# Gate and up weights in 512 x 256 blocks, and prefix counts laid out by expert, in a two-layer MoE backbone

## The chip, the cores and the metric

The kernel runs on one core of one Trainium2 chip. The metric is device microseconds (us) for one execution of the whole program; less is better. Engines: PE (TensorE), DVE (VectorE), ACT (ScalarE), POOL (GpSimd), SP (the queue that issues most transfers).

## What is computed

Two layers over 2048 latent and 256 context tokens of width 1024. Each layer has an attention half and then an expert-choice MoE half, cut here to what matters:

```
aff = softmax(h @ w_router)                 # 16 experts
gate, idx = top_k(aff^T, cap)               # per expert: 256 latent tokens, 32 context tokens
xe = h[idx]                                 # gather
a = xe @ w_gate[e];  u = xe @ w_up[e]       # 1024 x 512 each
y = (silu(a) * u) @ w_down[e] * gate        # 512 x 1024
out = zeros.at[idx].add(y)                  # scatter-add
```

Context tokens take part in layer 0 only. All of it is float32, with products made of three float32r products (high x high, low x high, high x low).

## The kernel before

The program is recorded in one order; each engine runs its own instructions in that order, and a waiting instruction holds all those behind it on its engine.

**Weights** come through `Stream` (lines 111 to 221). A block is 128 partitions x 1024 float32, 512 KB. `_load` (L163) issues its transfer on SP into `wraw`; `_high` (L178) makes the high part `wh` on ACT; `_low` (L186) makes the low part `wl` on DVE and thereby frees the `wraw` buffer, of which there are six, for the next transfer. `next(key, ahead=6)` makes sure that the high parts of the six blocks behind the wanted one have been recorded:

```
        while len(self.split) <= min(i + ahead, self.end - 1):
            ...
            self._high()
```

So an ACT cast of a block stands in ACT's order when the block six places ahead of it is used, and everything that ACT does after it waits for that block's transfer.

**One expert** (loop at L1790) uses twelve blocks: for each of four column blocks of 128 a gate block and an up block, eight matmul triples each into the PSUM tiles `pa` and `pu` (L1802 to L1804), and then four down blocks (L1833 to L1840). A block of gate or up is 1024 rows x 128 columns, so that each run in DRAM is 512 bytes. `tick()` (after each of these blocks) lets waiting tasks record their next step: `act` (silu on ACT, product on DVE, `gh` on ACT, `gl` on DVE), `trans(e + 1)` (transposes of the next expert's gathered tokens on PE, L1571; `xh` on ACT, L1580; `xl` on DVE, L1584; two PSUM buffers `tr`), `choose(e + 2)` and `put` (gated rows, scatter-add by POOL, L1666).

**The prefix counts.** `route` writes, once a layer, for each expert the running count of chosen tokens, 2048 bf16 values, to DRAM (`PFX`, L1499; `PFC` for the context tokens). They lie as [8 pieces, 16 experts, 256]. `fetch(e)` (L1518) copies the 4096 bytes of one expert to all 128 partitions of `pb`: 512 KB written, in runs of 512 bytes. `choose(e)` compares them with the slot numbers (L1530, two passes of DVE), makes the token numbers `ix`, and POOL gathers the rows `xe` (L1546). `pb` has two buffers; `fetch(e + 1)` is issued at the end of `choose(e)` on SP, between the weight blocks.

At the start of each MoE half the order is route, fetch(0), fetch(1), choose(0), gather, transposes, first expert. In layer 0, PE meanwhile works on modulation columns (`mod_piece`, L393). Late in layer 1 the finishing tasks (`fin_tile`, L1742 to L1774: two ACT passes and two DVE passes of 1024 columns a tile, L1769 and L1773) run beside the last three experts, one step a tick, and after them.

Of the kernel before, what the change touches and what calls it, by code (L numbers as in the profile page):

```python
# [7 lines left out]
F32 = mybir.dt.float32  # L8
F32R = mybir.dt.float32r
BF = mybir.dt.bfloat16  # L10
I32 = mybir.dt.int32
AF = mybir.ActivationFunctionType
# [11 lines left out]
KD = D // 128  # L24
NE = 16
CAP = 256
CCAP = 32
# [54 lines left out]
STEP = object()  # L82
# [142 lines left out]
def build(ctx, tc, t, out):  # L225
    nc = tc.nc
    V, S, P, G, SY = nc.vector, nc.scalar, nc.tensor, nc.gpsimd, nc.sync
# [4 lines left out]
    T = Tasks()  # L232
    W = Stream(nc, tc, T)

    def bcast(ap, n=128):
        return bass.AP(tensor=ap.tensor, offset=ap.offset, ap=[[0, n], *ap.ap])
# [31 lines left out]
    def dr(name, shape, dt=F32):  # L268
        return [dram.tile(shape, dt, name=f"{name}{i}") for i in range(DEPTH)]
# [10 lines left out]
    H2 = [dram.tile([n, HX], F32, name=f"H2{n}") for n in (TT, SEQ)]  # L280
    ACC = dr("ACC", [SEQ, D])
    ACCC = dram.tile([CTX, D], F32, name="ACCC")
    PFX = dr("PFX", [8, NE, 256], BF)
    PFC = dr("PFC", [8, NE, 32], BF)
    X1 = dram.tile([TT, D], F32, name="X1")

    def xrows(l, i):
# [10 lines left out]
    def k8(w):  # L298
        return w.rearrange("(k p) c -> p k c", p=128)

    def whole(a):
        return lambda x: x.rearrange("p (k c) -> p k c", k=a)
# [4 lines left out]
    def add_mod(l, j, kind="split", halves=(0, 1)):  # L307
        for b in halves:
            W.add(("mod", l, j, b), [(whole(4), k8(t["w_mod"][l][512 * b:512 * b + 512, 256 * j:256 * (j + 1)]))], kind)

    def mod_beside(l, e):

        j = NMOD + e - 1
        return j if l == 0 and 1 <= e and j < NLATE else None
# [23 lines left out]

    def add_moe(l):
        for e in range(NE):  # L340
            for f in range(4):
                for z in "gu":
                    W.add((z, l, e, f), [(whole(8), k8(t["w_gate" if z == "g" else "w_up"][l, e][:, 128 * f:128 * (f + 1)]))])
                if f in (1, 2) and mod_beside(l, e) is not None:
                    add_mod(1, mod_beside(l, e), halves=(f - 1,))
            for j in range(2):
                for b in range(2):
                    W.add(("d", l, e, j, b), [(whole(2), k8(t["w_down"][l, e][256 * b:256 * b + 256, 512 * j:512 * (j + 1)]))])
# [1078 lines left out]
    def route(l, aff, sb, ps):  # L1427


        last = l == DEPTH - 1  # L1430
# [25 lines left out]
        for it in range(15):  # L1456
# [9 lines left out]
            pc = ps.tile([128, 512], F32, name="py")  # L1466
# [29 lines left out]
        V.tensor_copy(need[:, 2, :], pc[:, 0:nj])  # L1496
        for j, s in enumerate(parts):
            V.tensor_tensor_scan(px[:, s], gt[:, s], gt[:, s], need[:, 2, j:j + 1], ALU.add, ALU.bypass)
            SY.dma_start((PFX, PFC)[j][l].rearrange("a e n -> (a e) n"), px[:, s])  # L1499
        yield  # L1500


    def phase_moe(l, aff):
        es = ExitStack()
        last = l == DEPTH - 1
# [9 lines left out]
        def fetch(e):  # L1515

            pb = sb.tile([128, SEQ], BF, name="pb")
            SY.dma_start(pb.rearrange("p (a n) -> p a n", a=8), bcast(PFX[l][:, e, :]))  # L1518
            pc = None
            if not last:  # L1520
                pc = sb.tile([CCAP, 256], BF, name="pc")
                SY.dma_start(pc.rearrange("p (a n) -> p a n", a=8), bcast(PFC[l][:, e, :], CCAP))
            prefixes[e] = pb, pc

        def choose(e):
# [98 lines left out]
            fp = es.enter_context(tc.tile_pool(name="fin", bufs=1))  # L1624
            fg, fb = load_ln2(l, fp)

        def act(ff, pa, pu, gh, gl):
            yield STEP
            sa = sb.tile([128, NX], F32, name="sa", bufs=3)
            S.activation(sa, pa, AF.Silu)  # L1630
            yield
            V.tensor_tensor(sa, pu, sa, op=ALU.mult)
            yield
            S.copy(gh[:, ff, :NX], sa)
            yield
            yield
            V.tensor_tensor(gl[:, ff, :], sa[:, :CAP], gh.bitcast(F32)[:, ff, :CAP], op=ALU.subtract)
            if not last:
                V.tensor_tensor(gh[:, ff, NX:NX + CCAP], sa[:, CAP:], gh.bitcast(F32)[:, ff, CAP:NX], op=ALU.subtract)
# [43 lines left out]
        def tick():  # L1683
            T.tick()
            F.tick()
# [28 lines left out]
        def fin_early():  # L1714
            for _ in range(FINLAG):
                yield STEP
            for n in range(14 + 2 * FINK):
                e = E0 + (n - 16) // 2
                while n >= 16 and e not in flags:
                    yield STEP  # L1720
                yield from fin_next()
                if n < 16:
                    SY.dma_start(xs[n], ACC[1][128 * n:128 * n + 128, :])
                else:
                    fin_gather(e, n % 2, xs[n])
                F.add(fin_tile(n))
                for _ in range(1 if "end" in flags else FINSTEP if NE - 2 not in flags else FINSTEP2):
                    yield STEP
# [61 lines left out]
        for e in range(NE):  # L1790
            xh, xl, gates = xT[e]
            gh = one.tile([128, 4, CAP + 2 * CCAP], F32R, name="gh")
            gl = one.tile([128, 4, CAP], F32R, name="gl")
            for j in range(2):
                for f in range(2):
                    pa = ps.tile([128, NX], F32, name="pa")
                    pu = ps.tile([128, NX], F32, name="pu")
                    for pp, z in ((pa, "g"), (pu, "u")):
                        wh, wl = W.next((z, l, e, 2 * j + f), ahead=6)
                        for k in range(KD):  # L1800
                            cs_ = slice(128 * k, 128 * k + 128)
                            P.matmul(pp, wh[:, cs_], xh[:, k, :], start=(k == 0), stop=False)  # L1802
                            P.matmul(pp, wh[:, cs_], xl[:, k, :], start=False, stop=False)  # L1803
                            P.matmul(pp, wl[:, cs_], xh[:, k, :], start=False, stop=(k == KD - 1))  # L1804
                        if z == "g":
                            tick()
                    if mod_beside(l, e) is not None and 2 * j + f in (1, 2):
                        if j == 0:
                            piece = mod_piece(1, mod_beside(l, e), ps, sb, True, "py", 2, apart=True,
                                              room=lambda: sb.tile([128, NX], F32, name="sa", bufs=3))  # L1810
                        next(piece)
                    T.add(act(2 * j + f, pa, pu, gh, gl), True)
                    if j == 0 and f == 0 and e + 1 < NE:
                        T.add(trans(e + 1))
                    if last and j == 0 and f == 0 and e == E0:
                        F.add(fin_early())
                    if j == 1 and f == 0 and e + 2 < NE:
                        T.add(choose(e + 2))
                    tick()
            ys = {}  # L1820
            for j in range(2):
                pys, ws = {}, {}

                def down(a, f):
                    if a not in pys:
                        pys[a] = ps.tile([128, 512], F32, name="py")
                    if f // 2 not in ws:
                        ws[f // 2] = W.next(("d", l, e, j, f // 2))
                    s_ = slice(512 * (f % 2), 512 * (f % 2) + 512)
                    wh, wl = (z[:, s_] for z in ws[f // 2])  # L1830
                    if a < 2:
                        h, lo = (z[:, f, 128 * a:128 * a + 128] for z in (gh, gl))
                        P.matmul(pys[a], h, wh, start=(f == 0), stop=False)  # L1833
                        P.matmul(pys[a], h, wl, start=False, stop=False)
                        P.matmul(pys[a], lo, wh, start=False, stop=(f == 3))
                    else:

                        P.matmul(pys[a][:2 * CCAP], gh[:, f, CAP:CAP + 2 * CCAP], wh, start=(f == 0), stop=False,
                                 skip_group_check=True)
                        P.matmul(pys[a][:CCAP], gh[:, f, CAP:CAP + CCAP], wl, start=False, stop=(f == 3),  # L1840
                                 skip_group_check=True)

                if j == 0:
                    for a in range(2):
                        for f in range(3):
                            down(a, f)
                        tick()
                for a in range(2 if last else 3):
                    for f in range(3 if j == 0 and a < 2 else 0, 4):
                        down(a, f)  # L1850
                    T.add(put(e, 128 if a < 2 else CCAP, a, j, pys[a], ys, gates), True)
                    tick()
# [99 lines left out]
```

## Time and profile before

| | us |
|---|---|
| median of 3 runs | 4326.2 (4321.42 to 4334.8) |
| profiled execution, its own time | 4323.15 |
| its span, first to last instruction | 4321.4 |
| PE busy | 3853.9 (89%) |
| DVE busy | 2915.8 (67%) |
| ACT busy | 1999.0 (46%) |
| mean granted TensorE clock | 0.943 |

The time is that of the device; the span is that of the records within it. Times in rows are us from the span's start. Busy shares are means over stages with different limits. Layer 0's experts run from 1487.3 to about 2178 with the last one behind, layer 1's from 3570.5 to about 4259.

### The profile page before, as it was taken

The page shows a single profiled execution, that of the slowest core. Times are in us where ns is not written, and L with a number is a line of the kernel's source. Part 1 is how long each engine was busy: PE and PEld are TensorE (multiplying, and loading weights), DVE is VectorE, ACT ScalarE, POOL GpSimd, SP SyncE. Part 2 cuts the span into 40 slices and gives each one's busy share as a digit, 9 for nine tenths or more (in the row PEclk, how much of TensorE's full clock was granted, in tenths as well). Part 3 has the DMA queues.
Part 4 walks back from the last instruction along what each step waited for, and adds up shares of the span by engine and source line. Part 5 has one row for each costly group of instructions (what it writes and reads, how often), then busy time and mean ns, then how long its engine had stood idle before and what let it go on. Part 6 is the DMA issues. An engine that isn't in the chain of part 4 may idle for free. (4 is left out here: it accounts for less than half of the span.)

```text
span 4321.4 us, 64189 instructions
## 1 busy us (share of the span) xinstructions
PE 3853.9 (89%) x22980; PEld 3285.1 (76%) x22980; DVE 2915.8 (67%) x5836; ACT 1999.0 (46%) x3918; POOL 783.9 (18%) x850
## 2 busy tenths in 40 slices
PE   7999989999998699999978999899989918988893
PEld 5877778888885388888857888788878718888783
DVE  6555549998676366676747665499877756656576
ACT  4344338887332143343425443388763304333344
POOL 0000011052221022222210000111422201111114
PEclk9999989999998899999989999999999959999996
DMA  7666674586644878888857666645865327776796
GB/s 229 172 209 187 198 189 107 118 177 154 235 159 143 189 208 201 204 217 196 223 171 230 192 205 187 171 116 110 169 185 193 131 80 190 195 221 194 217 234 203
DMA packets 897295, 789.94 MB, mean 183 GB/s; under 512 B 125928, under 2 KB 780400, under 8 KB 893136
## 3 DMA queue, kind: packets, MB, share of 16 engines
q1 hardware_dynamic: 855744, 656.83, 56.4%
q0 software_dynamic: 41232, 129.01, 10.6%
q8 instruction: 182, 2.98, 0.3%
q14 instruction: 137, 1.12, 0.1%
HBM read 607.08 MB, written 178.48 MB: 182 GB/s over the span
## 5 line engine op out<-in xcount | busy, mean ns | idle before, releaser
L178 ACT CAST wh<-wraw 128x1024 fp32r<-128x1024 f32 x636 | 655.9, 1048 | 621.9 <-DMA wraw<-in_w_gate 278.2
L186 DVE TENSOR_TENSOR wl<-wraw,wh 128x1024 fp32r<-128x1024 f32 x636 | 754.7, 1217 | 152.2 <-ACT wh L178 152.0
L1190 DVE TENSOR_TENSOR pl<-pt,ph 128x256 fp32r<-128x256 f32 (+2 forms) x792 | 360.2, 495 | 23.0 <-ACT ph L1199 18.4
L1199 ACT CAST ph<-pt 128x256 fp32r<-128x256 f32 (+2 forms) x792 | 308.9, 445 | 99.2 <-PE pt L1087 91.3
L624 PE MATMUL gem<-hh,wh 128*128 128x512 f32 (+1 forms) x960 | 354.5, 369 | 0.0
L625 PE MATMUL gem<-hl,wh 128*128 128x512 f32 (+1 forms) x960 | 352.1, 367 | 0.0
L626 PE MATMUL gem<-hh,wl 128*128 128x512 f32 (+1 forms) x960 | 350.0, 365 | 0.0
L1070 ACT ACTIVATE p<-lg,mx 128x640 f32<-128x640 f32 (+3 forms) x408 | 331.5, 813 | 38.3 <-DVE mx L1062 36.7
L1802 PE MATMUL pa<-xh,wh 128*128 128x288 f32 (+1 forms) x1024 | 317.5, 310 | 0.0
L1804 PE MATMUL pa<-xh,wl 128*128 128x288 f32 (+1 forms) x1024 | 308.3, 301 | 0.8 <-DVE wl L186 0.8
L1803 PE MATMUL pa<-xl,wh 128*128 128x288 f32 (+1 forms) x1024 | 307.3, 300 | 0.0
L1802 PE MATMUL pu<-xh,wh 128*128 128x288 f32 (+1 forms) x1024 | 299.9, 293 | 0.0
L1804 PE MATMUL pu<-xh,wl 128*128 128x288 f32 (+1 forms) x1024 | 294.6, 288 | 0.0
L1803 PE MATMUL pu<-xl,wh 128*128 128x288 f32 (+1 forms) x1024 | 292.6, 286 | 0.0
L1666 POOL DMA_INDIRECT ACC<-y,ix x62 | 150.7, 2430 | 651.7 <-DVE y L1647 334.2
L802 PE MATMUL gem<-wh,hh 128*128 128x512 f32 x544 | 220.7, 406 | 0.6 <-ACT hh L593 0.6
L803 PE MATMUL gem<-wl,hh 128*128 128x512 f32 x544 | 217.6, 400 | 1.4 <-DVE wl L186 1.4
L804 PE MATMUL gem<-wh,hl 128*128 128x512 f32 x544 | 217.0, 399 | 0.0
L1833 PE MATMUL py<-wh,gh 128*128 128x512 f32 x512 | 205.1, 401 | 12.7 <-DVE y L1647 6.1
L1571 PE MATMUL tr<-ident,xe 128*128 128x128 f32 x512 | 89.6, 300 | 139.4 <-DVE xl L1584 91.8
L1802 PEld LDWEIGHTS pa<-xh,wh 128*128 128x128 f32 x1024 | 208.5, 204 | 3.1
L1546 POOL DMA_INDIRECT xe<-H,ix x80 | 98.2, 1228 | 619.9 <-DVE ix L1541 352.9
(352 smaller groups left out, 10103.4 us busy)
## 6 DMA issues: line engine op xcount, KB each, us to landing
wraw<-in_w_in SPq DMA_DIRECT2D x160, 512.0 KB
wraw<-in_w_gate SPq DMA_DIRECT2D x128, 512.0 KB
wraw<-in_w_up SPq DMA_DIRECT2D x128, 512.0 KB
wraw<-in_w_down SPq DMA_DIRECT2D x128, 512.0 KB
wraw<-in_w_mod SPq DMA_DIRECT2D x88, 512.0 KB
k<-KC SPq DMA_DIRECT2D x48, 576.0 KB
vw<-VS SPq DMA_DIRECT2D x192, 128.0 KB
VS<-vs SPq DMA_DIRECT2D x36, 512.0 KB
```

Source lines behind the costliest of these rows:

```text
L178: self.nc.scalar.copy(h, self.raw[i])
L186: self.nc.vector.tensor_tensor(e[1], self.raw[i], e[0].bitcast(F32), op=ALU.subtract)
L624: P.matmul(pg[:, t0:nt], wh[:, cs_], hh[:, k, t0:nt], start=(k == 0), stop=False)
L625: P.matmul(pg[:, t0:nt], wh[:, cs_], hl[:, k, t0:nt], start=False, stop=False)
L626: P.matmul(pg[:, t0:nt], wl[:, cs_], hh[:, k, t0:nt], start=False, stop=(k == KD - 1))
L802: P.matmul(pg, hh[:, k, tk], wh[:, cs_], start=(k == 0), stop=False)
L1070: S.activation(p[:, 0:768 - w0], rec["lg"][:, w0:768], AF.Exp, bias=st[b]["mx"][:, m:m + 1], scale=-1.0, accum_out=st[b]["ss"][:, m:m + 1])
L1190: V.tensor_tensor(view(st[b]["pl"]), src, view(st[b]["ph"].bitcast(F32)), op=ALU.subtract)
L1199: S.copy(view(st[b]["ph"]), src)
L1802: P.matmul(pp, wh[:, cs_], xh[:, k, :], start=(k == 0), stop=False)
L1803: P.matmul(pp, wh[:, cs_], xl[:, k, :], start=False, stop=False)
L1804: P.matmul(pp, wl[:, cs_], xh[:, k, :], start=False, stop=(k == KD - 1))
```

## The change

Gate and up blocks become 512 rows x 256 columns: still 512 KB and twelve blocks an expert, but runs of 1024 bytes in DRAM. Two blocks, rows 0 to 511 and 512 to 1023, are now needed for two column blocks of 128, so two `pa` (or two `pu`) are summed side by side: gate first, then up, in each half `j` of the columns. `act` is split: `silu` is recorded behind each gate column block, the rest behind each up column block. There are five ticks in a half where there were four, and `trans(e + 1)` and `choose(e + 2)` are added one block earlier. The counts lie as [16 experts, 8 pieces, 256]: the write goes out with the pieces apart, and a fetch reads 4096 contiguous bytes for each partition.

```
-    PFX = dr("PFX", [8, NE, 256], BF)
+    PFX = dr("PFX", [NE, 8, 256], BF)
...
-            for f in range(4):
+            for j in range(2):
                 for z in "gu":
-                    W.add((z, l, e, f), [(whole(8), k8(t["w_gate" if z == "g" else "w_up"][l, e][:, 128 * f:128 * (f + 1)]))])
...
+                    w = t["w_gate" if z == "g" else "w_up"][l, e]
+                    for b in range(2):
+                        W.add((z, l, e, j, b), [(whole(4), k8(w[512 * b:512 * b + 512, 256 * j:256 * j + 256]))])
...
-            SY.dma_start((PFX, PFC)[j][l].rearrange("a e n -> (a e) n"), px[:, s])
+            SY.dma_start((PFX, PFC)[j][l].rearrange("e a n -> a e n"), px[:, s])
...
-            SY.dma_start(pb.rearrange("p (a n) -> p a n", a=8), bcast(PFX[l][:, e, :]))
+            SY.dma_start(pb, bcast(PFX[l][e].rearrange("a n -> (a n)")))
...
             for j in range(2):
...
+                for z in "gu":
+                    pp = [ps.tile([128, NX], F32, name=f"p{'a' if z == 'g' else 'u'}") for _ in range(2)]
+                    for b in range(2):
+                        wh, wl = W.next((z, l, e, j, b), ahead=6)
+                        for f in range(2):
+                            for k in range(4):
...
+                                P.matmul(pp[f], wh[:, cs_], xh[:, kk, :], start=(kk == 0), stop=False)
+                                P.matmul(pp[f], wh[:, cs_], xl[:, kk, :], start=False, stop=False)
+                                P.matmul(pp[f], wl[:, cs_], xh[:, kk, :], start=False, stop=(kk == KD - 1))
+                            if b:
+                                T.add(silu(2 * j + f, pp[f], sas) if z == "g" else
+                                      act(2 * j + f, sas[2 * j + f], pp[f], gh, gl), True)
+                                if z == "u" and f == 0:
+                                    tick()
+                        if b == 0 and z == "g":
+                            if j == 0 and e + 1 < NE:
+                                T.add(trans(e + 1))
...
+                            if j == 1 and e + 2 < NE:
+                                T.add(choose(e + 2))
+                        if b == 0 or z == "u":
                             tick()
```

The program has as many PE, POOL and weight-transfer instructions as before. How they stand in three places:

**SP, one expert of layer 1.** `wraw` rows are weight transfers (partitions x pieces x columns), `pb` is the fetch. Before:

```order
L163 DMA wraw<-in_w_gate 128x8x128
L163 DMA wraw<-in_w_up 128x8x128
L1518 DMA pb<-PFX_105 128x8x256
L163 DMA wraw<-in_w_gate 128x8x128
L163 DMA wraw<-in_w_up 128x8x128
L163 DMA wraw<-in_w_down 128x2x512 x4
```

And with the change (the fetch is L1520 there):

```order
L163 DMA wraw<-in_w_gate 128x4x256 x2
L163 DMA wraw<-in_w_up 128x4x256 x2
L163 DMA wraw<-in_w_gate 128x4x256
L1520 DMA pb<-PFX_105 128x2048
L163 DMA wraw<-in_w_gate 128x4x256
L163 DMA wraw<-in_w_up 128x4x256 x2
L163 DMA wraw<-in_w_down 128x2x512 x4
```

The fetch stands ahead of the last three gate and up transfers of an expert where it stood ahead of the last two; it has one piece to a partition where it had eight.

**ACT, the end of one expert's up blocks and the start of the next expert, layer 1.** Before (`sa<-pa` is silu, `gh` the high part for the down product, `xh` the next expert's tokens):

```order
L178 CAST wh<-wraw 128x1024
L1630 ACTIVATE sa<-pa 128x256
L1634 CAST gh<-sa 128x256
L178 CAST wh<-wraw 128x1024 x7
L1630 ACTIVATE sa<-pa 128x256
L1580 CAST xh<-tr 128x512
```

With the change (silu is L1632, `gh` L1639, `xh` L1582):

```order
L1632 ACTIVATE sa<-pa 128x256 x2
L178 CAST wh<-wraw 128x1024
L1639 CAST gh<-sa 128x256 x2
L178 CAST wh<-wraw 128x1024 x6
L1582 CAST xh<-tr 128x512
L178 CAST wh<-wraw 128x1024
```

Both last `gh` casts of an expert now stand together behind a weight cast, and the next expert's first `xh` stands behind six weight casts where it stood behind seven and a silu.

**DVE, from one expert's last rows to the next expert's first `xl`, layer 1.** Before:

```order
L186 TENSOR_TENSOR wl<-wraw,wh 128x1024 x2
L1647 SCALAR_TENSOR_TENSOR y<-py,gates,g_35803 128x512
L186 TENSOR_TENSOR wl<-wraw,wh 128x1024 x4
L1632 TENSOR_TENSOR sa<-pu,sa 128x256
L1637 TENSOR_TENSOR gl<-sa,gh 128x256
L1584 TENSOR_TENSOR xl<-tr,xh 128x512
```

With the change (`y` is L1652, `xl` L1586, the product L1637):

```order
L186 TENSOR_TENSOR wl<-wraw,wh 128x1024 x2
L1652 SCALAR_TENSOR_TENSOR y<-py,gates,g_35803 128x512
L186 TENSOR_TENSOR wl<-wraw,wh 128x1024 x3
L1586 TENSOR_TENSOR xl<-tr,xh 128x512
L186 TENSOR_TENSOR wl<-wraw,wh 128x1024
L1586 TENSOR_TENSOR xl<-tr,xh 128x512
L186 TENSOR_TENSOR wl<-wraw,wh 128x1024
L1637 TENSOR_TENSOR sa<-pu,sa 128x256
```

On PE the four groups of transposes for the next expert stand behind 24, 48, 72 and 84 of an expert's 192 gate and up matmuls, where they stood behind 48, 72, 96 and 120. At the program's end, eight rows of the first finishing pass (L1769) stand on DVE behind the last `y` row, not counting those of the last expert's own tiles; before there were eleven.

## Rows read from the trace of the kernel before

**Rows 1.** Windows: the expert stretches, the end; engines busy, granted clock, DMA share, GB/s.
```profile
core 0: us, PE busy (x) PEld busy (x) DVE busy (x) ACT busy (x) POOL busy (x), PEclk, DMA share, GB/s
3570.50:3608.00 37.50, 37.36 (x259) 34.82 (x258) 27.53 (x39) 20.42 (x29) 3.80 (x3) 0.96 0.48 138
...
3608.00:4213.60 605.60, 533.96 (x3587) 492.58 (x3586) 384.41 (x517) 242.31 (x356) 87.99 (x62) 0.94 0.81 214
4213.60:4252.00 38.40, 30.59 (x219) 28.22 (x218) 23.75 (x34) 19.85 (x33) 11.13 (x14) 0.96 0.80 236
4252.00:4321.40 69.40, 6.89 (x23) 5.12 (x21) 42.42 (x66) 27.63 (x46) 39.66 (x42) 0.55 0.54 185
```

**Rows 2.** Waits, fourteen experts of layer 1: us in total, times, longest.
```profile
ACT wh L178 <- DMA wraw<-in_w_gate: 161.5, 13, 13.9
...
PE tr L1571 <- DVE xl L1584: 63.0, 14, 5.3
```

**Rows 3.** Timeline, one expert of layer 1, SP.
```profile
3810.30 0.58 SPq L1518 DMA_DIRECT2D pb<-PFX  x1
3812.32 0.37 SPq L163 DMA_DIRECT2D wraw<-in_w_gate  x1
```

**Rows 4.** Timeline, the same place, ACT; in brackets the idle time before.
```profile
3831.21 1.05 ACT L178 CAST wh<-wraw 128x1024 fp32r<-128x1024 f32 x1 [12.41 <-DMA wraw<-in_w_gate]
...
3838.97 0.58 ACT L1580 CAST xh<-tr 128x512 fp32r<-128x512 f32 x1
```

**Rows 5.** Timeline, the same place, PE.
```profile
3841.08 1.11 PE L1571 MATMUL tr<-ident,xe 128*128 128x128 f32 x4 [4.96 <-DVE xl L1584]
```

**Rows 6.** Windows, the same place, columns as in rows 1.
```profile
3815.00:3827.00 12.00, 11.86 (x66) 9.91 (x65) 7.40 (x8) 3.06 (x4) 2.34 (x1) 1.00 0.20 39
...
3834.00:3844.00 10.00, 5.04 (x33) 4.84 (x32) 5.66 (x8) 6.39 (x10) 1.59 (x1) 0.79 1.08 329
```

**Rows 7.** Windows in which one kind of transfer runs, columns as in rows 1.
```profile
3526.00:3538.00 12.00, 0.00 (x0) 0.00 (x0) 0.00 (x0) 0.00 (x0) 0.00 (x0) 0.50 0.23 47
3474.30:3476.50 2.20, 0.27 (x2) 0.27 (x2) 1.81 (x10) 1.32 (x2) 0.24 (x1) 0.50 0.90 279
3928.00:3931.00 3.00, 3.00 (x16) 3.00 (x16) 2.53 (x5) 1.84 (x5) 0.00 (x0) 0.50 1.12 300
2194.00:2197.00 3.00, 3.00 (x25) 3.00 (x24) 0.91 (x1) 0.41 (x1) 0.00 (x0) 1.00 1.07 362
```

**Rows 8.** Timeline, head of layer 1, SP: a row of 4096 bytes to all partitions.
```profile
3473.24 0.32 SPq L1617 DMA_DIRECT2D g<-MODR  x1
```

**Rows 9.** Timeline, head of layer 1, SP: the first fetches.
```profile
3525.14 18.93 SPq L1518 DMA_DIRECT2D pb<-PFX  x3
```

**Rows 10.** Timeline, head of layer 1, DVE.
```profile
3538.94 2.35 DVE L1530 TENSOR_SCALAR_CACHE_REDUCE junkb<-pb,slotc 128x2048 bf16<-128x2048 bf16 x1 [15.38 <-DMA pb<-PFX]
```

**Rows 11.** Timeline, head of layer 1, POOL and its last gather of the first expert.
```profile
3546.08 0.96 POOL L1546 DMA_INDIRECT xe<-H,ix  x1 [0.30 <-issue]
```

**Rows 12.** Timeline, head of layer 1, PE.
```profile
3565.01 0.45 PE L1571 MATMUL tr<-ident,xe 128*128 128x128 f32 x1 [42.43 <-DMA xe<-H,ix]
```

**Rows 13.** Transfers of fourteen experts, layer 1: count and us to landing.
```profile
xe<-H,ix POOLq DMA_INDIRECT x26, 6.2
```

**Rows 14.** Timeline, head of layer 0, DVE.
```profile
1450.60 2.35 DVE L1530 TENSOR_SCALAR_CACHE_REDUCE junkb<-pb,slotc 128x2048 bf16<-128x2048 bf16 x1 [15.89 <-DMA pb<-PFX]
```

**Rows 15.** Timeline, head and first expert of layer 0, PE.
```profile
1453.17 0.34 PE L406 MATMUL pa<-ident,mrow 2*128 2x2 f32 x2 [14.18 <-DVE modc L417]
...
1516.22 1.11 PE L1571 MATMUL tr<-ident,xe 128*128 128x128 f32 x4 [10.84 <-DVE xl L1584]
```

**Rows 16.** Windows, first four experts of layer 0 and eleven after, columns as in rows 1.
```profile
1487.30:1548.50 61.20, 49.17 (x282) 44.20 (x282) 35.22 (x58) 21.09 (x29) 10.63 (x5) 0.83 0.74 178
...
1645.40:1695.10 49.70, 45.75 (x282) 41.30 (x281) 31.27 (x51) 19.26 (x28) 13.19 (x6) 0.93 0.88 201
1695.10:2178.20 483.10, 473.34 (x3082) 424.94 (x3081) 338.04 (x550) 200.70 (x298) 124.86 (x63) 1.00 0.85 208
```

More of the change, by code (lines that the diff above doesn't have):

```diff
@@ L282, in build @@
     ACCC = dram.tile([CTX, D], F32, name="ACCC")
-    PFX = dr("PFX", [8, NE, 256], BF)
-    PFC = dr("PFC", [8, NE, 32], BF)
+    PFX = dr("PFX", [NE, 8, 256], BF)
+    PFC = dr("PFC", [NE, 8, 32], BF)
     X1 = dram.tile([TT, D], F32, name="X1")
@@ L340, in add_moe @@
         for e in range(NE):
-            for f in range(4):
+            for j in range(2):
                 for z in "gu":
-                    W.add((z, l, e, f), [(whole(8), k8(t["w_gate" if z == "g" else "w_up"][l, e][:, 128 * f:128 * (f + 1)]))])
-                if f in (1, 2) and mod_beside(l, e) is not None:
-                    add_mod(1, mod_beside(l, e), halves=(f - 1,))
+                    w = t["w_gate" if z == "g" else "w_up"][l, e]
+                    for b in range(2):
+                        W.add((z, l, e, j, b), [(whole(4), k8(w[512 * b:512 * b + 512, 256 * j:256 * j + 256]))])
+                    if (j, z) in ((0, "u"), (1, "g")) and mod_beside(l, e) is not None:
+                        add_mod(1, mod_beside(l, e), halves=(j,))
             for j in range(2):
@@ L1521, in fetch @@
                 pc = sb.tile([CCAP, 256], BF, name="pc")
-                SY.dma_start(pc.rearrange("p (a n) -> p a n", a=8), bcast(PFC[l][:, e, :], CCAP))
+                SY.dma_start(pc, bcast(PFC[l][e].rearrange("a n -> (a n)"), CCAP))
             prefixes[e] = pb, pc
@@ L1625, in phase_moe, with silu, act @@
             fg, fb = load_ln2(l, fp)
-        def act(ff, pa, pu, gh, gl):
+        def silu(ff, pa, sas):
             yield STEP
-            sa = sb.tile([128, NX], F32, name="sa", bufs=3)
-            S.activation(sa, pa, AF.Silu)
+            sas[ff] = sb.tile([128, NX], F32, name="sa", bufs=3)
+            S.activation(sas[ff], pa, AF.Silu)
             yield
+        def act(ff, sa, pu, gh, gl):
+            yield STEP
             V.tensor_tensor(sa, pu, sa, op=ALU.mult)
@@ L1793, in phase_moe @@
             gl = one.tile([128, 4, CAP], F32R, name="gl")
+            sas = {}
             for j in range(2):
[L1795 to L1805, printed above, removed]
+                for z in "gu":
[4 more added lines that the diff above has]
+                            for k in range(4):
+                                kk = 4 * b + k
+                                cs_ = slice(256 * k + 128 * f, 256 * k + 128 * f + 128)
+                                P.matmul(pp[f], wh[:, cs_], xh[:, kk, :], start=(kk == 0), stop=False)
[9 more added lines that the diff above has]
+                                T.add(trans(e + 1))
+                            if last and j == 0 and e == E0:
+                                F.add(fin_early())
+                            if j == 1 and e + 2 < NE:
+                                T.add(choose(e + 2))
+                        if b == 0 or z == "u":
@@ L1806, in phase_moe @@
                             tick()
-                    if mod_beside(l, e) is not None and 2 * j + f in (1, 2):
+                    if (j, z) in ((0, "u"), (1, "g")) and mod_beside(l, e) is not None:
                         if j == 0:
@@ L1811, in phase_moe @@
                         next(piece)
[L1812 to L1819, printed above, removed]
+                    if z == "g":
+                        tick()
             ys = {}
```

## The prediction

> **What bounds the kernel now.** I read the page first: PE is busy 89% of the span, so a gain has to come from where PE stands or runs at the lower clock. The change touches only the two MoE halves, so I cut these into windows of one expert each, then asked for the waits of such a window, then for the timeline around the longest.
>
> Layer 1 first. Its fourteen experts after the first take 605.6 us, 43.3 each, with PE busy 534.0 and a mean granted clock of 0.94; the first expert, whose weights were loaded before it began, does the same work in 37.5 us, busy 37.4, with the DMA engines only 0.48 busy [rows 1]. So these experts lose some 6 us each to something that the first does not have. The waits name it: once in nearly every expert ACT stands for a gate block (161.5 us in 13 times), and PE stands behind `xl` (63.0 us in 14 times) [rows 2]. The timeline of one expert joins the two. SP issues the fetch of the prefix counts at 3810.30 and the next gate block at 3812.32 [rows 3]; that block is cast only at 3831.21, after 12.41 us of waiting, and the next expert's `xh`, behind it on ACT, only at 3838.97 [rows 4]; PE, which needs `xl` to have its `tr` buffer back, stands 4.96 us [rows 5]. All that time the DMA engines are nearly empty: from 3815 to 3827 they are busy 0.20 and move 39 GB/s, and the granted clock in the window that holds PE's stop is 0.79, so part of it is at the lower level of 1.2 GHz [rows 6].
>
> What moves at 39 GB/s is the fetch. At the head of layer 1, where fetches are alone, they move 47 GB/s [rows 7], that is 524 KB in 11.2 us. The weight blocks behind it in SP's queue cannot pass it.
>
> Layer 0 has the same fetch, but more columns for PE: eleven of its experts take 483.1 us, 43.9 each, at full clock with PE busy 473.3, so the late block hides there. Its first four take 207.8 us, the first alone 61.2 at a clock of 0.83 [rows 16].
>
> **The change, part by part.** *The fetch.* It becomes one run of 4096 bytes to each partition. The kernel has that transfer already: L1617 spreads a row of 4096 bytes over 128 partitions. It is issued at 3473.24 [rows 8] and its window, to 3476.5, shows 279 GB/s [rows 7]: 1.9 us of transfer, 3.3 us from the issue. A fetch gets 9.3 us shorter. This is a transfer of the same shape, so I take it whole; the other end is no gain.
>
> *The weight blocks.* Runs of 512 bytes move at 300 GB/s, modulation blocks with runs of 1024 bytes at 362 [rows 7]: 1.75 against 1.45 us a block, 2.4 us of DMA time an expert over eight blocks. With the fetch that is 11.7 us an expert, about the 12.41 that ACT waits.
>
> The Trainium skill ("DMA: Bandwidth & Descriptors", Specifications) gives 512 bytes as the least transfer for line rate. By that rule both old forms run at full rate and the change gives nothing, 4323 us; the rows differ from it, mildly for the weights and by a factor of six for the fetch.
>
> *Layer 1, experts 1 to 14.* With the blocks on time an expert should look like the first: 37.5 us, of which its own clock of 0.96 cost 1.5, so 36.0 at best [rows 1]. I take 37.5, leaving those 1.5 us for small new waits: 14 x (43.26 - 37.5) = 81 us. Bounds: 14 x 7.26 = 102 if nothing new waits; 40 if half of the loss stays.
>
> *Head of layer 1.* The first fetch is issued at 3525.14 [rows 9] and used at 3538.94 [rows 10]: 13.8 us, now 3.3, so 10.5 saved, with PE idle throughout. Then the two gathers: the last is issued at 3546.08 [rows 11] and lands for PE at 3565.01 [rows 12], 18.9 us, while the second and third fetch hold the DMA queues; a gather in the expert stretch lands in 6.2 [rows 13]. Together 23 us. I take 20, since two bias rows go out in the same time; bounds 10 and 24.
>
> *Head of layer 0.* DVE waits 15.89 us for the first fetch [rows 14], and PE 14.18 behind DVE [rows 15]. The same 10.5 us come off; I take 10. Bounds: 4, if the modulation blocks that PE then needs are late in turn, and 19, if the second fetch's share comes off too.
>
> *First four experts of layer 0.* At the pace of the later ones they would take 4 x 43.9 = 176 instead of 208 [rows 16], less what two modulation pieces need, which no row separates. PE's longest stop there, 10.84 us, is again `xl` [rows 15]. I take 18; bounds 0 and 30.
>
> *The other experts of layer 0.* PE is idle 9.8 us in eleven [rows 16]; I take 3, with bounds of 10 gained and 10 lost to new waits.
>
> *Last expert and end.* 38.4 and 69.4 us [rows 1]. Two more ticks an expert push the finishing tasks on: eight of their passes stand behind the last `y` row instead of eleven. They then compete with faster experts, so I take 4; bounds -5 and 12.
>
> *What the new order costs.* Reading `pa` early and the extra ticks add no work: PE has the same matmuls. The transposes stand 24 to 36 matmuls earlier, but the first `xh` also stands one weight cast earlier, so their distance to the transfers stays about the same. Shorter is the way from the last but one up column block to the down product: 12 matmuls and the first down ones, where there were 36 more. It is covered as long as the weight cast ahead of `gh` on ACT does not wait; its block is the next expert's second gate block, ahead of the fetch in the queue. I cost it at nothing in the steady stretch; without the cover it is the second rival.
>
> Sum: 81 + 20 + 10 + 18 + 3 + 4 = 136 us. From the profiled execution's 4323.15 us (span 4321.4) that is 4187; the median of the runs is 3 us higher, and I forecast 4188. A change of 0.3%, 13 us, is about what can be told from none here.
>
> **The rivals.** *The next bound is close behind.* DVE is busy 384 of 606 us in layer 1's stretch [rows 1], 27.5 us an expert, and works in order; at 37.5 us it is three quarters full, and each `wl` that is late frees its `wraw` buffer late. If an expert then takes 40, the largest term is 46 instead of 81 and the heads and first experts give 30 of their 48: 4323 - 46 - 30 - 7 = 4240. For it: every stop of PE in that stretch is at the end of an ACT and DVE chain. Against it: the first expert has the same chain and 37.5. Chance 0.2.
>
> *Slower: the down product waits.* If ACT's weight cast ahead of the last `gh` pair waits as long as it now does once an expert (12.4 us), PE, covered by some 3 us of matmuls, stops 9 us in each of 32 experts. It decides from 136 / 32 = 4.3 us an expert on; at 9 us the time is 4323 - 136 + 290 = 4477. Against it: the block that waits now is the one right behind the fetch [rows 3, 4], and the one ahead of `gh` is not. Chance 0.03.
>
> *The fetch stays slow* because 128 partitions read the same bytes, whatever the run. Only 2.4 us an expert then come off in layer 1 and part of it in layer 0: about 34 + 10, so 4280. Against it: L1617 does just that at 279 GB/s. Chance 0.04.
>
> *Nothing, by the line-rate rule, or because transfers are hidden*: 4323. Against it: PE's stops lie under these waits. Chance 0.03.
>
> *More than forecast*: all terms near their upper bounds, 102 + 24 + 19 + 25 + 5 + 10 = 185, so 4138. Chance 0.1.
>
> **Numbers.** The forecast itself, 4150 to 4222, has 0.6. Range: 4138 to 4250, from the better case to just past the near bound, which leaves out parts of it and the last three kinds. Faster by over 0.3%: 0.6 + 0.2 + 0.1 + 0.04 = 0.94. Same: 0.03. Slower: 0.03.
>
> **What would show it.** In the changed profile: a window with fetches alone at over 200 GB/s; no wait of ACT for a gate block over some 3 us in layer 1's stretch; PE's wait for `xl` there under 15 us in total; experts at 36 to 39 us with a clock near 1.00; the first gather of layer 1 landing some 20 us sooner after the route. I am wrong if fetches still move at some 50 GB/s, or if PE stops at the first down product (`py`) or at `pu` instead, or if experts of layer 1 stay over 41 us with the queues empty.

## The result, and the profile after

The changed kernel takes 4169.99 us (median, 4169.93 to 4174.62) where the kernel before took 4329.94 in the same job: a ratio of 0.9636, with a 95% interval of 0.9619 to 0.9653. The span fell from 4321.4 to 4168.1 us, by 153.3.

From the page of the changed kernel, the busy times of the engines and the packets:

```profile
PE 3816.9 (92%) x22980; PEld 3252.6 (78%) x22980; DVE 2906.3 (70%) x5836; ACT 2007.4 (48%) x3918; POOL 826.0 (20%) x850
DMA packets 733942, 789.93 MB, mean 190 GB/s; under 512 B 121808, under 2 KB 612952, under 8 KB 729784
```

The same bytes go in 18% fewer packets, and PE has the same 22980 matmuls. Windows of the changed kernel, columns as in rows 1: the first four experts of layer 0 and the other eleven, then in layer 1 the first expert, the next twelve, experts 13, 14 and 15, and the end.

```profile
1473.60:1654.90 181.30, 179.14 (x1158) 160.28 (x1159) 133.13 (x222) 81.60 (x117) 57.52 (x23) 0.98 0.74 221
1654.90:2128.40 473.50, 471.81 (x3082) 425.11 (x3082) 336.78 (x550) 202.58 (x297) 135.65 (x63) 1.00 0.73 210
...
3499.60:3536.90 37.30, 37.16 (x259) 34.61 (x258) 27.33 (x39) 21.47 (x29) 5.23 (x3) 0.96 0.56 184
3536.90:3969.20 432.30, 430.57 (x3074) 400.06 (x3073) 320.14 (x433) 203.42 (x288) 93.73 (x49) 1.00 0.84 249
3969.20:4011.30 42.10, 37.41 (x258) 34.54 (x257) 29.36 (x43) 22.39 (x34) 9.27 (x9) 0.96 0.81 251
4011.30:4059.00 47.70, 40.82 (x258) 36.56 (x257) 32.39 (x47) 23.35 (x38) 7.69 (x11) 0.89 0.80 243
4059.00:4099.00 40.00, 28.86 (x206) 27.45 (x205) 22.11 (x33) 19.11 (x32) 9.61 (x12) 0.88 0.70 211
4099.00:4168.00 69.00, 9.00 (x37) 6.60 (x35) 41.37 (x64) 25.25 (x42) 38.27 (x40) 0.60 0.46 167
```

Set against the boundaries in [rows 1, 16], the 153.3 us fall into the terms of the prediction's sum:

| stretch | before | after | gained | forecast |
|---|---|---|---|---|
| start to the first expert of layer 0 | 1487.3 | 1473.6 | 13.7 | 10 |
| its first four experts | 207.8 | 181.3 | 26.5 | 18 |
| its other eleven | 483.1 | 473.5 | 9.6 | 3 |
| from there to the end of layer 1's first expert | 1429.8 | 1408.5 | 21.3 | 20 |
| layer 1, experts 1 to 14 | 605.6 | 522.1 | 83.5 | 81 |
| last expert and end | 107.8 | 109.1 | -1.3 | 4 |

The head of layer 1 shows the fetch: SP's issue, DVE's first use of the counts, POOL's second gather, and PE's first transpose.

```profile
3476.88 9.22 SPq L1520 DMA_DIRECT2D pb<-PFX  x3
3481.00 2.35 DVE L1532 TENSOR_SCALAR_CACHE_REDUCE junkb<-pb,slotc 128x2048 bf16<-128x2048 bf16 x1 [6.29 <-DMA pb<-PFX]
3488.15 0.97 POOL L1548 DMA_INDIRECT xe<-H,ix  x1 [0.30 <-issue]
3494.40 0.45 PE L1573 MATMUL tr<-ident,xe 128*128 128x128 f32 x1 [20.67 <-DMA xe<-H,ix]
```

From issue to use the fetch takes 4.12 us instead of 13.80 [rows 9, 10], and the gather behind it 6.25 instead of 18.9 [rows 11, 12]. A window with nothing else in it, and ACT's wait for gate blocks in the twelve experts:

```profile
3477.00:3481.00 4.00, 0.00 (x0) 0.00 (x0) 0.00 (x0) 0.00 (x0) 0.00 (x0) 0.50 0.76 235
```
```profile
ACT wh L178 <- DMA wraw<-in_w_gate: 38.6, 13, 4.1
```

So 235 GB/s in place of 47 [rows 7], and a longest wait of 4.1 us in place of 13.9 [rows 2]; PE no longer waits for `xl` there at all. From expert 13 to the end of PE's work other waits stand:

```profile
ACT junkb L1753 <- DMA fx<-ACC: 41.8, 8, 9.1
...
PE py L1846 <- ACT gh L1639: 10.8, 2, 6.9
...
PE pu L1809 <- DVE sa L1637: 7.0, 2, 4.2
PE py L1846 <- DVE y L1652: 7.0, 3, 4.7
```

`fx` is a tile of finished rows that the finishing tasks (LayerNorm of the output) load. ACT works in order, and while it stands for `fx`, `gh` and the weight casts stand behind it, and PE behind these. These waits are longer, not new: the kernel before had them too, from 4169 us on, that is in its last two experts.

```profile
ACT junkb L1748 <- DMA fx<-ACC: 26.6, 7, 10.6
...
PE py L1833 <- DVE y L1647: 6.1, 3, 3.4
...
PE py L1833 <- ACT gh L1634: 4.6, 2, 4.5
```

Now they begin in expert 13, and PE's stops at `pu` have come to them.

### The profile page after: what moved, and what is told of

Its sections match the earlier page's. It is cut to its first block, busy times and chain, and to the rows that moved or that the text cites. A ratio compares the mean times of both kernels' runs of the same rounds, so it can differ in the third digit from the quotient of the medians.

```text
span 4168.1 us, 64121 instructions
## 1 busy us (share of the span) xinstructions
PE 3816.9 (92%) x22980; PEld 3252.6 (78%) x22980; DVE 2906.3 (70%) x5836; ACT 2007.4 (48%) x3918; POOL 826.0 (20%) x850
## 5 line engine op out<-in xcount | busy, mean ns | idle before, releaser
L1192 DVE TENSOR_TENSOR pl<-pt,ph 128x256 fp32r<-128x256 f32 (+2 forms) x792 | 359.9, 494 | 21.3 <-ACT ph L1201 16.8
L1809 PE MATMUL pa<-xh,wh 128*128 128x288 f32 (+1 forms) x1024 | 300.5, 293 | 0.7 <-DVE modc L419 0.7
L1811 PE MATMUL pa<-xh,wl 128*128 128x288 f32 (+1 forms) x1024 | 296.7, 290 | 0.8 <-DVE wl L186 0.8
L1810 PE MATMUL pa<-xl,wh 128*128 128x288 f32 (+1 forms) x1024 | 294.0, 287 | 0.0
L1548 POOL DMA_INDIRECT xe<-H,ix x80 | 161.7, 2021 | 476.3 <-DVE ix L1543 398.3
L1671 POOL DMA_INDIRECT ACC<-y,ix x62 | 128.8, 2077 | 579.6 <-DVE y L1652 326.9
L626 PEld LDWEIGHTS gem<-hh,wh 128*128 128x128 f32 x960 | 182.7, 190 | 31.4
L628 PEld LDWEIGHTS gem<-hh,wl 128*128 128x128 f32 x960 | 182.7, 190 | 31.1
```

The costliest lines, as they stand in the source:

```text
L626: P.matmul(pg[:, t0:nt], wh[:, cs_], hh[:, k, t0:nt], start=(k == 0), stop=False)
L628: P.matmul(pg[:, t0:nt], wl[:, cs_], hh[:, k, t0:nt], start=False, stop=(k == KD - 1))
L1192: V.tensor_tensor(view(st[b]["pl"]), src, view(st[b]["ph"].bitcast(F32)), op=ALU.subtract)
L1809: P.matmul(pp[f], wh[:, cs_], xh[:, kk, :], start=(kk == 0), stop=False)
L1810: P.matmul(pp[f], wh[:, cs_], xl[:, kk, :], start=False, stop=False)
L1811: P.matmul(pp[f], wl[:, cs_], xh[:, kk, :], start=False, stop=(kk == KD - 1))
```

## The experiments

Once both traces were read I held **theory A**: the slow fetch is the whole cause, the weight tiles and the new order are worth nothing by themselves. Rivals: **B**, the weight tiles and the order bring part of the gain; **C**, both are needed together. What makes the fetch slow was a question of its own.

**1. Counts alone.** The kernel before with the counts by expert; gate and up blocks and their order as before.

```
-    PFX = dr("PFX", [8, NE, 256], BF)
+    PFX = dr("PFX", [NE, 8, 256], BF)
...
-            SY.dma_start(pb.rearrange("p (a n) -> p a n", a=8), bcast(PFX[l][:, e, :]))
+            SY.dma_start(pb, bcast(PFX[l][e].rearrange("a n -> (a n)")))
```

> The kernel before with the counts laid out by expert alone; weight blocks, order and ticks as before. Theory A (the fetch holds the queue, and nearly all the gain is its own): the fetch falls from 11 us to 2, layer 1's experts come down to 36 to 38 us, and the time is 4165 to 4200. Rival B (the weight blocks' run length is needed as well, because 512-byte runs leave the queue too full): experts of layer 1 stay at 39 to 41 us and the time is 4220 to 4260. Rival C (the new order of the blocks did it): under 20 us gained, 4310 or more.

Measured: 4158.36 us, ratio 0.9611 [0.959, 0.9631]. The whole gain is there, without the weight tiles, and the time is somewhat below the 4165 that I had put as A's least. The fetch at the head of layer 1, SP and DVE:

```profile
3468.79 9.07 SPq L1518 DMA_DIRECT2D pb<-PFX  x3
3472.77 2.35 DVE L1530 TENSOR_SCALAR_CACHE_REDUCE junkb<-pb,slotc 128x2048 bf16<-128x2048 bf16 x1 [6.14 <-DMA pb<-PFX]
```

The fetch is used 3.98 us after its issue. A holds, B and C fall.

**2. Weight tiles and order alone.** The changed kernel with the counts laid out and fetched as before (the edit of experiment 1, turned round).

> The changed kernel with the counts laid out as before: new blocks and order, old fetch. Theory A: the fetch still takes 11 us and ACT still waits for a gate block in each expert of layer 1; only the shorter blocks come off, 2.4 us an expert there, so 4270 to 4310. Rival B: the larger part of the 160 us, 4200 to 4240. A third way: with the transposes standing earlier, the late block costs PE more than before, and the time is 4330 to 4350.

Measured: 4363.67 us, ratio 1.0071 [1.0047, 1.0095]: slower than before, and slower than any of the forecasts, though the third of them had the way right. In layer 1 the waits (3600 to 4130 us), and one of PE's stops in its timeline, show a new place:

```profile
ACT wh L178 <- DMA wraw<-in_w_gate: 144.5, 14, 13.4
...
PE tr L1573 <- DMA xe<-H,ix: 91.8, 14, 43.5
```
```profile
3706.48 0.55 PE L1573 MATMUL tr<-ident,xe 128*128 128x128 f32 x3 [3.83 <-DMA xe<-H,ix]
```

One of the 14 is the head of the layer, 43.5 us; the other 13 are 48.3 us, 3.7 each. Before, PE stopped for `xl` [rows 5]; here it stops earlier, for the gathered rows. The transposes stand 24 to 36 matmuls earlier in the new order, and the rows are chosen only once the fetch has landed. So the prediction's "their distance to the transfers stays about the same" is good only with a fast fetch. Long weight runs do not make up for it.

**3 and 4. Shorter runs, near each other.** Is it the 512 bytes of a piece? The changed kernel with an expert's counts as eight pieces of 512 bytes, 1024 apart (experiment 3), and as two pieces of 2048 bytes, 4096 apart (experiment 4, with two writes instead of one).

```
-    PFX = dr("PFX", [NE, 8, 256], BF)
+    PFX = dr("PFX", [NE, 8, 512], BF)
...
-            SY.dma_start(pb, bcast(PFX[l][e].rearrange("a n -> (a n)")))
+            SY.dma_start(pb.rearrange("p (a n) -> p a n", a=8), bcast(PFX[l][e, :, 0:256]))
```

> The changed kernel, but an expert's eight pieces lie 1 KB apart in DRAM, so that a fetch again reads eight runs of 512 bytes for each partition, close together. If the run's length makes the fetch slow: 40 to 60 GB/s where fetches are alone, and 4270 to 4310 like the old layout with the new blocks. If the 8 KB between the pieces made it slow: over 200 GB/s and 4165 to 4180.

> The changed kernel with each expert's counts as two pieces of 2048 bytes, 4 KB apart: two runs for each partition. If a fetch costs by its number of runs (1024 runs in 11.2 us, so some 90 in a us): 256 runs in 2.8 us, 180 GB/s alone, and 4168 to 4185. If only one single contiguous run escapes the slow way: 40 to 60 GB/s and over 4260.

Measured: 4167.96 us, ratio 0.963 [0.9611, 0.9648], and 4170.65 us, ratio 0.9632 [0.9616, 0.9649]: both as the changed kernel. In experiment 3 the fetch is used 3.87 us after its issue:

```profile
3469.33 9.00 SPq L1520 DMA_DIRECT2D pb<-PFX  x3
3473.20 2.35 DVE L1532 TENSOR_SCALAR_CACHE_REDUCE junkb<-pb,slotc 128x2048 bf16<-128x2048 bf16 x1 [6.05 <-DMA pb<-PFX]
```

Run length is not the cause: the old pieces of 512 bytes are as fast, if they lie close. What was left is where they lie: 8192 bytes apart. In experiment 4, with its two pieces 4096 bytes apart, the fetch is used 4.15 us after its issue:

```profile
3475.92 9.27 SPq L1524 DMA_DIRECT2D pb<-PFX  x3
3480.07 2.35 DVE L1536 TENSOR_SCALAR_CACHE_REDUCE junkb<-pb,slotc 128x2048 bf16<-128x2048 bf16 x1 [6.89 <-DMA pb<-PFX]
```

**5 and 6. The distance.** The kernel before with one unused row in each piece, so that the pieces stand 8704 bytes apart (experiment 5); and the changed kernel with an expert's pieces 8192 bytes apart but no other expert's between them (experiment 6, the edit of experiment 3 with 4096 for 512).

```
-    PFX = dr("PFX", [8, NE, 256], BF)
+    PFX = dr("PFX", [8, NE + 1, 256], BF)
...
-            SY.dma_start((PFX, PFC)[j][l].rearrange("a e n -> (a e) n"), px[:, s])
+            SY.dma_start((PFX[l][:, 0:NE], PFC[l])[j], px[:, s])
```

> The kernel before, with one unused row of 512 bytes behind the sixteen experts' rows in each of the eight pieces of the prefix counts: an expert's eight pieces of 512 bytes then lie 8704 bytes apart instead of 8192; weights and order as before. Theory P (what slows the fetch is the distance of exactly 8192 bytes, a power of two, at which all eight pieces fall on the same part of the memory): the fetch at the head of layer 1 is used some 4 to 5 us after its issue instead of 13.8, and the kernel comes near the one with only the counts rearranged (4158): 4150 to 4175. Theory Q (pieces that lie far apart are slow at any such distance): 13 to 14 us as before, 4315 to 4340.

> The changed kernel, with each expert's counts cut into eight pieces of 512 bytes that lie 8192 bytes apart, the experts behind one another. The same run with 1024 bytes between the starts was fast. Theories P and Q both: the fetch at the head of layer 1 takes 13 to 14 us from issue to use again, and the time is that of the new weights with the old counts, 4345 to 4375. If instead it was slow because the experts' rows lie between one another, or because of how they were written: 4 to 6 us, 4160 to 4180.

Measured: experiment 5, 4150.4 us, ratio 0.958 [0.956, 0.9601]; experiment 6, 4350.31 us, ratio 1.0047 [1.0032, 1.0061]. Experiment 5, the packets of the page, then SP and DVE at the head of layer 1:

```profile
DMA packets 897279, 789.94 MB, mean 190 GB/s; under 512 B 125912, under 2 KB 780384, under 8 KB 893120
```
```profile
3476.36 8.97 SPq L1518 DMA_DIRECT2D pb<-PFX  x3
3480.20 2.35 DVE L1530 TENSOR_SCALAR_CACHE_REDUCE junkb<-pb,slotc 128x2048 bf16<-128x2048 bf16 x1 [6.01 <-DMA pb<-PFX]
```

Practically the packets of before (897295 there), and 4.2% of the time gone. Experiment 6, the same two, and a window with the fetch alone:

```profile
3553.37 18.80 SPq L1520 DMA_DIRECT2D pb<-PFX  x3
```
```profile
3567.05 2.35 DVE L1532 TENSOR_SCALAR_CACHE_REDUCE junkb<-pb,slotc 128x2048 bf16<-128x2048 bf16 x1 [15.93 <-DMA pb<-PFX]
```
```profile
3554.00:3566.00 12.00, 0.00 (x0) 0.00 (x0) 0.00 (x0) 0.00 (x0) 0.00 (x0) 0.50 0.62 48
```

13.68 us and 48 GB/s, as before. P's forecast holds and Q falls: far apart is not slow as such, since 8192 bytes are slow and 8704 are not. The reason that P gives, that the pieces fall on the same part of the memory, no run shows.

**12. A distance of 4096.** The changed kernel, eight pieces of 512 bytes, 4096 apart (2048 for 512 in experiment 3's edit), run once.

> The changed kernel with eight pieces of 512 bytes 4096 bytes apart (1024 apart was fast, 8192 apart slow, 8704 apart fast). If only the distance of 8192 bytes is bad: the fetch at the head of layer 1 is used about 4 us after its issue, 4160 to 4180. If smaller powers of two are bad in part: 7 to 11 us, 4200 to 4330.

Measured: 4193.51 us in its one run. SP and DVE:

```profile
3487.99 14.99 SPq L1520 DMA_DIRECT2D pb<-PFX  x3
3497.85 2.35 DVE L1532 TENSOR_SCALAR_CACHE_REDUCE junkb<-pb,slotc 128x2048 bf16<-128x2048 bf16 x1 [12.08 <-DMA pb<-PFX]
```

9.86 us: slow in part, so 8192 is not alone. Nor is the distance: experiment 4 had the same 4096 bytes between two pieces of 2048 and took 4.15 us. Whether the number of pieces or their length makes that difference was not tried. Yet twelve experts of layer 1 still run without a stop, and most of the loss against the changed kernel is at the heads. I had put 4200 as the least for this case; a fetch of 9.9 us still fits into an expert, one of 13.8 does not.

**9. The weights' run length.** The changed kernel with each gate or up block loaded as two transfers of 128 columns. (The weights are float32, so a run is 512 bytes again instead of 1024.)

```
-                        W.add((z, l, e, j, b), [(whole(4), k8(w[512 * b:512 * b + 512, 256 * j:256 * j + 256]))])
+                        W.add((z, l, e, j, b), [(part(4, 128 * c, 128 * c + 128), k8(w[512 * b:512 * b + 512, 256 * j + 128 * c:256 * j + 128 * c + 128])) for c in range(2)])
```

> The changed kernel, order and counts as there, but each gate and up block of 512 rows by 256 columns is loaded as two transfers of 128 columns each, into the same places: runs of 256 columns by 2 bytes, 512 bytes, become half as long... in the kernel's 32-bit weights 1024 bytes become 512 again, as before the change, with eight more DMA issues an expert. Theory W (the run length of the weights is worth nothing once the fetch is fast, since the blocks are in time anyway): experts of layer 1 stay at 36.0 us and the time is 4160 to 4180. Rival V (the longer runs are what gives the queues their slack): experts at 37 to 39 us, 4190 to 4230.

Measured: 4174.45 us, ratio 0.9644 [0.9626, 0.9663], not to be told from the changed kernel. The window of twelve experts of layer 1:

```profile
3535.90:3967.90 432.00, 430.27 (x3072) 399.75 (x3072) 319.95 (x432) 203.15 (x288) 92.95 (x49) 1.00 0.93 249
```

The DMA share is 0.93 where the changed kernel has 0.84 at the same 249 GB/s. Over 432 us that is 39 us of DMA time, 3.2 an expert. The edit also doubles the number of transfers, but experiment 1, with the old blocks in one transfer each, has 0.91 at the same 249 GB/s in its twelve experts (3529 to 3961 us), some 2.5 us an expert. So the longer runs are cheaper, about as costed (2.4). But nobody waits for it: W holds, V falls.

**10. Finishing tasks held back.** The changed kernel with `FINLAG = 1000` for 4, so that no finishing task starts before the last expert's matmuls are issued.

> The changed kernel with the finishing tasks of layer 1 held back until the last expert's matmuls are issued; they then all stand at the end. Theory F2 (the stops of PE in experts 13 to 15 come from the finishing tasks, not from the new order or the weights): experts 13 and 14 take 36.0 us like the others instead of 42.1 and 47.7, the last one 37 to 40, and the end grows by more than that, 30 to 90 us, so that the time is 4190 to 4240. Rival H (the stops come from the end of the weight stream or from the new order): experts 13 and 14 stay over 40 us.

Measured: 4186.94 us, ratio 0.9674 [0.9654, 0.9694]. Windows of experts 13, 14, 15 and the end:

```profile
3964.90:4000.80 35.90, 35.76 (x258) 33.22 (x257) 26.67 (x37) 16.87 (x24) 7.46 (x5) 1.00 0.78 236
4000.80:4036.90 36.10, 35.96 (x258) 33.42 (x257) 22.21 (x31) 16.85 (x24) 4.02 (x3) 1.00 0.70 204
4036.90:4072.90 36.00, 34.19 (x241) 31.30 (x239) 19.19 (x30) 9.35 (x15) 5.51 (x5) 1.00 0.64 190
4072.90:4183.30 110.40, 0.00 (x0) 0.00 (x0) 58.14 (x88) 49.04 (x82) 49.16 (x59) 0.51 0.51 176
```

Without them all three experts take 36 us: PE's stops there come from the finishing tasks (F2). They cost 21.8 us in the three experts (129.8 against 108.0) and take 41.4 off the end (69.0 against 110.4), so that holding them back loses less than F2's least (4190).

**7, 8 and 11. Shifting them.** Experiment 7 is the changed kernel with the extra tick between two up blocks moving the expert's own tasks only. Experiment 8 is the kernel of experiment 1 with `FINGO = 4`, not 2, ticks between a finishing load and ACT's pass. Experiment 11 is the kernel of experiment 5 with `FINSTEP = 3` instead of 4.

```
-                                    tick()
+                                    T.tick()
```

> The changed kernel, but the extra tick in the middle of a pair of up blocks moves only the expert's own tasks on, not the finishing tasks. Theory F (the finishing pass on ACT comes a fixed count of ticks after its load was issued, the new tick made these shorter in time, and ACT now waits for the loaded rows with the casts and gh behind it): ACT's wait for fx falls from 41.8 us in 8 times in experts 13 to 15 to under 20, experts 13 and 14 fall from 42.1 and 47.7 to 37 to 41, and the time to 4150 to 4162; a part may come back behind the last expert, since fewer finishing passes are then done. Rival G (the stops come from what the finishing tasks ask of ACT, DVE and the DMA queues in sum, wherever they stand): 4164 to 4175.

> The kernel before with only the prefix counts by expert (4158 in its own run), and with 4 ticks instead of 2 between the load of a finishing tile and ACT's pass over it. Theory F: ACT's wait for fx nearly goes, expert 14 falls from 46.6 to 38 to 41 us, and the time is 4140 to 4153. Rival G: the pass only moves, and the time stays at 4154 to 4165.

> The kernel before with the padded prefix counts (4150), and finishing tiles begun every 3 ticks instead of 4 up to the last expert but one. If the end is bound by how many tiles are still to be finished behind the last matmul: the stretch behind it falls from 68.8 us by 3 to 8, 4142 to 4149. If the finishing work only moves into the experts, which then stop more: 4149 to 4165.

Measured: experiment 7, 4162.81 us, ratio 0.9604 [0.9577, 0.9632]; experiment 8, 4166.19 us, ratio 0.9619 [0.9595, 0.9643]; experiment 11, 4164.34 us, ratio 0.9623 [0.9601, 0.9645]. In 7, expert 13 is whole again, and ACT's wait for `fx` falls from 41.8 to 26.9 us; its windows of expert 13 and 14:

```profile
3971.90:4007.90 36.00, 35.85 (x257) 33.31 (x257) 26.92 (x41) 15.74 (x26) 7.26 (x6) 1.00 0.90 279
4007.90:4050.80 42.90, 37.82 (x258) 35.07 (x257) 32.07 (x45) 25.63 (x40) 7.26 (x10) 0.92 0.81 246
```

From expert 13 to the end that is 188.9 us against 198.8, but the intervals of the two kernels overlap, so the measured times alone do not confirm it; 4162.81 lies between the forecasts of F and G, and the wait did not fall under F's 20 us. Experiment 8 takes ACT's wait for `fx` almost away (3.5 us, where experiment 1 has 28.0) and shortens expert 14 (39.8 us, from 46.7). But from the start of the last expert on it takes 116.2 us, where experiment 1 takes 103.8, and the kernel was no faster than experiment 1. There DVE stands with its finishing pass for POOL's part of it (`fm`), the expert's product `sa` stands behind that pass, and PE behind `sa`:

```profile
4076.54 1.28 DVE L1773 SCALAR_TENSOR_TENSOR fx<-fx,fm,ln_b 128x1024 f32<-128x1024 f32 x1 [12.94 <-POOL fm L497]
...
4079.47 0.58 PE L1802 MATMUL pu<-xh,wh 128*128 128x256 f32 x1 [8.93 <-DVE sa L1632]
```

Experiment 11 shortens the end to 67.0 us (68.8 in experiment 5) and pays with 50.8 in expert 14 (45.2). So the finishing tasks stop PE (experiment 10), but ACT's wait for `fx` is only one way in which they do: without it PE stopped elsewhere. Experiments 8 and 11 moved the loss, as G had it; whether experiment 7 won its few us stays open.

## Why the prediction was right

- **What bounds it, the fetch.** Right, and stronger than put: experiments 1 and 5 bring the whole gain with nothing else changed. Its size was taken from L1617's row, 3.3 us from issue; it was 4.12, and 235 GB/s against 279. The 279 were misread: over 2.2 us they are 614 KB, more than L1617's 524, because a write of 128 KB by POOL (L1423, issued at 3473.34) ran in the same window. The 3.3 us do not hang on that. L1617 was the right row for a reason I did not have. I read it against the fetch as one run of 4096 bytes against pieces of 512; experiments 3, 5 and 6 show that for these pieces the distance decides. That the row fitted was in part luck: one unbroken run has neither short pieces nor a distance between them, so it could not tell the two apart.
- **The weight blocks.** The price was about right (2.4 us an expert; 3.2 by experiment 9, 2.5 by experiment 1), its place on the path was not. "With the fetch that is 11.7 us an expert, about the 12.41 that ACT waits" added a part that is hidden once the fetch is gone.
- **Layer 1, experts 1 to 14.** 83.5 against 81, and two errors in it cancel. Twelve experts run at 36.0 each instead of the 37.5 forecast, 18 us better (432.3 against 450); experts 13 and 14 take 89.8 instead of 75, 15 worse, by the finishing tasks.
- **Heads.** 13.7 and 21.3 against 10 and 20 (the second with the unchanged first expert). The gather lands in 6.25 us, as [rows 13] said.
- **First four experts of layer 0.** 26.5 against 18, inside the bounds. I could not separate the modulation pieces; the window now has PE busy 179.1 of 181.3.
- **Other experts of layer 0.** 9.6 against 3, at the upper bound: PE's idle time there fell from 9.8 to 1.7 us.
- **Last expert and end.** -1.3 against 4, inside its bounds: the competition that I named ate the gain. It begins two experts earlier than I put it.
- **The new order "costs nothing".** In the steady stretch yes (36.0 us with either order). Over the whole kernel the old order is no worse: experiment 5 has 0.958 [0.956, 0.9601] where the full change has 0.9636 [0.9619, 0.9653], each against the kernel before in its own job. Their profiles differ from expert 13 on: 198.8 us in the changed kernel, and in experiment 5 (expert 13, 14, 15, end) 189.3:

```profile
3969.50:4005.50 36.00, 35.85 (x258) 33.31 (x257) 28.39 (x40) 16.82 (x26) 5.55 (x7) 1.00 0.96 264
4005.50:4050.70 45.20, 37.89 (x258) 34.80 (x257) 31.60 (x46) 25.30 (x41) 7.76 (x8) 0.96 0.87 237
4050.70:4090.00 39.30, 31.78 (x222) 29.22 (x221) 24.29 (x36) 19.98 (x34) 11.16 (x14) 0.91 0.77 236
4090.00:4158.80 68.80, 6.37 (x21) 4.70 (x19) 41.91 (x64) 27.64 (x46) 39.71 (x42) 0.55 0.52 184
```

- **The rivals.** *The next bound is close behind*: no, twelve experts run at full clock with DVE busy 320 of 432 us. *The down product waits*: PE does stop at `py`, but in the last three experts, where the finishing tasks run. *The fetch stays slow* and *nothing*: out. *More than forecast*, 4138: the steady stretch went that way, the last experts took it back.

By the signs that I named: fetches over 200 GB/s, yes; ACT's gate wait no longer than some 3 us, nearly (4.1); PE's wait for `xl` under 15 us, yes; experts of 36 to 39 us, yes but for experts 13 to 15; the first gather some 20 us sooner, yes.

## What to carry to other kernels

When one transfer is slow, compare its rate with another of the same shape in the same trace, and then ask what else differs between the two: here bytes, packets and their lengths were equal in a fast and a slow form, and only the distance between the pieces was not. Where a transfer with large powers of two between its pieces is slow, try padding the distance before rewriting the layout; one unused row won here what the whole change won. (4096 and 8192 bytes were slow for eight pieces; 1024, a power of two as well, was fast.) And when a stretch gets faster, look again at what was timed by its ticks: work that was slipped in at fixed counts of ticks comes sooner, and its loads did not get faster (those of `fx` land in a median of 4.4 us before and after). Shifting it was worth nothing certain here.

## What the runs showed that I had not expected

How long after its issue a broadcast of eight 512-byte pieces to 128 partitions (524 KB) was first used went by the distance between the pieces: 3.87 us at 1024 bytes, 9.86 at 4096 (one run), 13.68 and 13.80 at 8192, 3.84 at 8704. One unbroken run of 4096 bytes to each partition took 4.12. The Trainium skill ("DMA: Bandwidth & Descriptors", Latency and other measured facts, its row on the pitch of rows in HBM at large powers of two) knows such a loss at pitches of 512 KiB and more, and padding as the cure, and calls its mechanism an inference; here the loss is seen at 4 and 8 KB and the cure at 8 KB, where all partitions read the same addresses. The distance does not act alone: two pieces of 2048 bytes, 4096 apart, took 4.15 us. What in the memory makes it so, no run here shows. Only 8704 was tried of the distances that are no power of two, so whether the power counts, or any multiple of 4096, is open. Nor was it tried whether one partition's fetch, or other lengths of piece 8192 bytes apart, are hit in the same way.
